# RMS norm of later queries and keys through a product with ones, ScalarE and GpSimd; modulation products spread over four FFN tiles

## The chip, the cores and the metric

The kernel runs on one core of a Trainium2 chip. The metric is the time of one execution on the device in microseconds (us), the median of several runs. A core has these engines: TensorE (PE, with its weight loads shown apart as PEld) multiplies matrices into PSUM; VectorE (DVE), ScalarE (ACT) and GpSimd (POOL) work elementwise; SyncE (SP) issues the DMAs here. Each engine works through its own queue in order and waits on semaphores for the others.

## The reference

Two layers work on 512 latent and 256 context tokens of width 1024. Layer 0 is grouped-query attention, layer 1 a bidirectional state-space mixer; behind each comes a gated FFN with a short convolution. Shift, scale and gate of each sub-layer come from `ada_w` and the condition vectors. The part that the change touches:

```python
def rms_norm(x, g):
    xf = x.astype(jnp.float32)
    y = xf * lax.rsqrt(jnp.mean(xf * xf, axis=-1, keepdims=True) + EPS)
    return (y * g.astype(jnp.float32)).astype(x.dtype)
...
    q_l, k_l, v_l = jnp.split(h_lat @ w_qkv, [Q_DIM, Q_DIM + KV_DIM], axis=-1)
    q_l = rms_norm(q_l.reshape(bsz, seq, N_HEADS, HEAD_DIM), q_norm)
    k_l = rms_norm(k_l.reshape(bsz, seq, N_KV_HEADS, HEAD_DIM), k_norm)
...
    q_l = apply_rope(q_l, cos, sin)
    k_l = apply_rope(k_l, cos, sin)
...
    for i in range(DEPTH):
        need_ctx_out = i < DEPTH - 1
        mod_l = jnp.split((silu_c @ ada_w[i] + ada_b[i])[:, None, :], 6, axis=-1)
        mod_c = jnp.split(silu_cc @ ada_w[i] + ada_b[i], 6, axis=-1)
```

There are 16 query heads and 4 key heads of 64; the norm runs over the 64 values of one head and token. EPS is 1e-6.

## The kernel before

Activations lie transposed: 128 features on the partitions, 768 tokens (512 latent, then 256 context) in the free dimension. A tile of 128 rows so holds two heads of 64 rows each. Linear layers run as three products in a reduced fp32 format: a weight tile and an activation are each split into a high and a low half (`split`, `load_w`: ACT makes the high half at L85, VectorE or GpSimd the low half at L87), and `mm3` adds high x high, high x low and low x high (L105 to L108).

The kernel is written for a framework that places instructions into the engines' queues at build time: by a priority, which is the order of the program's text, and by when it reckons that an instruction's inputs are ready. On the chip each queue then runs in this fixed order.

**Attention.** Eight pairs of heads `p` (one query tile each) go through seven steps each (`Pair.steps`): scores into PSUM (L668, L670), exponential on ACT (L671), sum of exponentials on VectorE (L678), and one step later the product with the values (L632). In the steps of pair p the maxima of pair p+1 are found too (`Pair.maxima`, L596 and L598), and for these the queries of pair p+1 must be normed and split. Scores and maxima share a PSUM ring of two buffers (`S`); all other products share four banks (`Bank`).

Into each step `Fill.run` puts other work from a queue of generators: the projection of later queries, their norm, the modulation products `ada` of layer 0 and, later, the output projection. A generator's `yield` says how much of the step's budget (1.75 us in pairs 0 to 5, 2.9 in 6 and 7) its piece used; a `yield BREAK` counts 1.0 and rests the generator until the third step after. `fill.require` (L738, L740) runs the rest of a generator on the spot if it isn't done when its pair needs it. The queue is written out as "123a4k5a6a7aaa" (L722): digits are queries, k the second tile of keys (needed from pair 3), a an `ada`.

**The norm.** `normed` (L520) squares the tile on ACT (`sq`, L523), applies the gain (L524), and rotates the positions: four DMAs on SP swap the rows (L527), and three operations on engine `eng` do the rotation (L528 to L530). `eng` is VectorE for key tile 0 and query tile 0, GpSimd for key tile 1 and query tiles 1 to 7. Then `rstd_rows` (L227): six small products with `blk`, which has one column for each head, put the sums of squares with tokens on the partitions (`ssq`, L236); VectorE scales them (L239); ACT takes Ln and Exp for the root (L241); VectorE makes one Newton step (L243, L244) and spreads the result over a head's 64 columns (`rbq`, L247); six transposes on TensorE bring it back to features on the partitions (`rsTq`, L253); VectorE multiplies (L534). The pieces are parted by BREAKs: three in a norm. Behind it `queries` splits the tile into `qh` and `ql` (L569), `keys` makes its copies (L545 to L548).

**FFN of layer 0 and the products of modulation.** `ffn` goes through 22 tiles `f` of the hidden width. `up(f)` makes two products (gate branch and up branch, each with its own weight), the convolution on VectorE (L832, L833), SiLU on ACT and the gating on VectorE (`hd`, L843), and its split (`hdh`, `hdl`). Tiles are collected in groups (3, then 2 at a time); the down-product of a group (`flush`, `down`) follows the first tile of the next group. Beside this runs the generator `side`, which is `ada_dve` (L153): the modulation of layer 0's FFN gate and of all of layer 1 as dot products on VectorE, 80 in all, each 1024 elements long (`junk`, L167). Each `next(side)` issues one. The first 16 make the gate that the first down-product's result is multiplied with (L779); a `modulation` (L145) follows them. `up(f)` takes `some` of them behind the SiLU and as many behind the second product (L835 to L840).

Of the kernel before, what the change touches and what calls it, by code (L numbers as in the profile page):

```python
# [7 lines left out]
P = 128  # L8
F32 = mybir.dt.float32
F32R = mybir.dt.float32r  # L10
AF = mybir.ActivationFunctionType
ALU = mybir.AluOpType
# [5 lines left out]
L = 512  # L18
C = 256
T = L + C  # L20
HD = 64
# [4 lines left out]
EPS = 1e-6  # L26
# [41 lines left out]
def t3(g, name, dt=F32, n=T):  # L68
    return g.t3p.tile([P, n], dt, tag="t3", bufs=g.n3, name=name)
# [103 lines left out]
BREAK = object()  # L173
# [53 lines left out]
def rstd_rows(g, sq, n, cols, width, name, bank):  # L227

    nc = g.nc
    c = cols.shape[-1]
    nt = n // P
    ps = bank(f"ss{name}")
    for t in range(nt):
        nc.tensor.matmul(ps[:, t * c : (t + 1) * c], sq[:, t * P : (t + 1) * P], cols, start=True, stop=True)  # L236
    small = lambda nm: g.p.tile([P, nt * c], F32, tag="rst", bufs=8, name=nm)
    a, y, u = small("rsa"), small("rsy"), small("rsu")
    nc.vector.tensor_scalar(a, ps[:, : nt * c], 1.0 / width, EPS, ALU.mult, ALU.add)  # L239

    for f in ((lambda: nc.scalar.activation(y, a, AF.Ln)), (lambda: nc.scalar.activation(y, y, AF.Exp, scale=-0.5))):  # L241
        follow(g, f()) if g.tables else f()
    nc.vector.tensor_tensor(u, y, a, ALU.mult)  # L243
    nc.vector.scalar_tensor_tensor(u, y, -0.5, u, ALU.mult, ALU.mult)  # L244
    rb = t3(g, f"rb{name}", n=n)
    wide = lambda v: v.unsqueeze(2).broadcast_to([P, nt * c, P // c])
    nc.vector.scalar_tensor_tensor(rb.rearrange("p (a b) -> p a b", b=P // c), wide(u), 1.5, wide(y), ALU.add, ALU.mult)  # L247
    yield BREAK
    out = []
    for t0 in range(0, nt, 4):  # L250
        pt = bank(f"rsT{name}")
        for t in range(t0, min(nt, t0 + 4)):
            nc.tensor.transpose(pt[:, (t - t0) * P : (t - t0 + 1) * P], rb[:, t * P : (t + 1) * P], g.ident)  # L253
        yield (pt, t0 * P, min(n, (t0 + 4) * P))
# [124 lines left out]
def attention(g, fill, X, late):  # L379


    nc, I = g.nc, g.I
    S64 = slice(0, 64), slice(64, 128)
# [123 lines left out]
    def values():  # L507
        for t in range(T // P):
# [7 lines left out]
                yield 0.32  # L516
            nc.scalar.copy(vt[t], ps[:, :256])


    def normed(qs, gain, eng):  # L520

        sq = t3(g, "qsq")
        nc.scalar.activation(sq, qs, AF.Square)  # L523
        nc.scalar.activation(qs, qs, AF.Identity, scale=gain)  # L524
        sw = t2("qsw")
        for b in range(4):
            nc.sync.dma_start(sw[32 * (b ^ 1) : 32 * (b ^ 1) + 32], qs[32 * b : 32 * b + 32, :L])  # L527
        eng.tensor_tensor(qs[:, :L], qs[:, :L], g.cos, ALU.mult)  # L528
        eng.tensor_tensor(sw, sw, g.sin, ALU.mult)
        eng.tensor_tensor(qs[:, :L], qs[:, :L], sw, ALU.add)  # L530
        for r in rstd_rows(g, sq, T, g.blk, HD, "q", Bk):
            if r is not BREAK:
                pt, c0, c1 = r
                nc.vector.tensor_tensor(qs[:, c0:c1], qs[:, c0:c1], pt[:, : c1 - c0], ALU.mult)  # L534
            yield BREAK
# [255 lines left out]
def ffn(g, layer, streams, x, h, first, nxt=None, side=iter(()), after=()):  # L791

    nc, I = g.nc, g.I
    ns = len(streams)
    tot = sum(n for n, _ in streams)
    off = [0, L]

    cw = [g.par[:, PC[f"fw{layer}{t}"] : PC[f"fw{layer}{t}"] + NFT] for t in range(3)]  # L800
    cb = g.par[:, PC[f"fb{layer}"] : PC[f"fb{layer}"] + NFT]
    whole = [[(i, 0, n) for i, (n, _) in enumerate(streams)]]

    def gemm(t):

        if t % NFT == 0:
            ps = first[t // NFT]
        else:
            w = load_w(g, I["wup"][layer, t])
            if t % NFT == 1:  # L810
                out = []
                for i in range(ns):
                    ps = Bank(g, "ps_up1")
                    for _ in gemm_in(g, [(ps, w)], h, (0, 0), [[s] for s in whole[0] if s[0] == i]):
                        pass
                    out.append((ps, [i]))
                return [(ps[:, : streams[i][0]], off[i], off[i] + streams[i][0], i) for ps, (i,) in out]
            ps = S(g, "ps_up")
            for _ in gemm_in(g, [(ps, w)], h, off, [[s] for s in whole[0]]):
                pass  # L820
        return [(ps[:, :tot], 0, tot, None)]

    def up(f):
        pg = gemm(f)
        cv = t3(g, "cv", n=tot)
        w0, w1, w2 = (c[:, f : f + 1] for c in cw)
        for ps, a, b, _ in pg:
            nc.scalar.activation(cv[:, a:b], ps, AF.Identity, scale=w1, bias=cb[:, f : f + 1])
        for i in range(ns):
            a, b = off[i], off[i] + streams[i][0]  # L830
            ps, o = next((ps, o) for ps, o, e, j in pg if j in (None, i))
            nc.vector.scalar_tensor_tensor(cv[:, a + 1 : b], ps[:, a - o : b - o - 1], w0, cv[:, a + 1 : b], ALU.mult, ALU.add)  # L832
            nc.vector.scalar_tensor_tensor(cv[:, a : b - 1], ps[:, a - o + 1 : b - o], w2, cv[:, a : b - 1], ALU.mult, ALU.add)  # L833
        follow(g, nc.scalar.activation(cv, cv, AF.Silu))
        some = 4 if ns > 1 and f < 2 else 1  # L835
        for _ in range(some):
            next(side, None)
        pu = gemm(NFT + f)
        for _ in range(some):
            next(side, None)  # L840
        hd = t3(g, "hd", n=tot)
        for ps, a, b, _ in pu:
            nc.vector.tensor_tensor(hd[:, a:b], cv[:, a:b], ps, ALU.mult)  # L843
        hi, lo = t3(g, "hdh", F32R, n=tot), t3(g, "hdl", F32R, n=tot)
        split(g, hd, hi, lo)
        return [(hi[:, off[i] : off[i] + streams[i][0]], lo[:, off[i] : off[i] + streams[i][0]]) for i in range(ns)]

    gate = g.mod[layer][5]
    segs, f = [], 0
    for n in [3] + [2] * 8 + [3] if nxt else [2] * 11:  # L850
        segs.append(range(f, f + n))
        f += n
    acts, pend, wf = {}, None, []

    def flush(fs, order, norm=None, after=None):
        ws = [load_w(g, I["wdown"][layer, f * P : (f + 1) * P]) for f in fs]
        if after:
            wf.extend(firsts(g, *after))
        return down(g, ws, [acts.pop(f) for f in fs], gate, streams, x, order, norm, side=side)

    for fs in segs:
        for j, f in enumerate(fs):
            acts[f] = up(f)
            if j == 0 and pend:
                flush(pend, whole)
        pend = fs
    for _ in side:
        pass
    if nxt:
        ln_exp(g)  # L870
    return flush(pend, [[s] for s in ending(streams)], nxt, after), wf
# [569 lines left out]
```

## Time and profile before

| | |
|---|---|
| Runs | 1917.7, 1918.88, 1925.51 us; median 1918.88 |
| Profiled execution | 1921.56 us, span of its trace 1919.8 us, mean granted TensorE clock 0.991 |
| TensorE, share of the span | 98% |
| VectorE | 68% |
| ScalarE | 43% |
| GpSimd | 16% |
| DMA, mean | 109 GB/s |

The attention stage lies at about 45 to 395 us, the FFN of layer 0 at about 445 to 965 us. In the rows, an operation stands with its line, its engine, its form (partitions x elements), its count, the time that the group kept the engine busy, the mean ns of one, and the idle time of the engine before it with what ended it. In the view of one tile three numbers are the least, the median and the longest ns. Rows of the timeline begin with start and length in us; those of the chain of waits too. TensorE's products overlap in its pipeline, so the length of one is longer than the distance to the next. A row of windows has the stretch, its length, the busy time of PE, PEld, DVE, ACT and POOL with the number of instructions, the granted clock, the DMA share and GB/s.

### The profile page before, as it was taken

To read this page: it belongs to the slowest core of one execution; us is meant where nothing else is said; L and a number is where in the kernel's file an instruction comes from. 1 tells how busy PE (TensorE), PEld (TensorE's weight loads), DVE (VectorE), ACT (ScalarE), POOL (GpSimd) and SP (SyncE) were. 2 spreads that over 40 slices of the span, in tenths; PEclk is the share of its full clock that TensorE was granted. 3 is DMA by queue.
4 is the path that set the end of the run, shared out by engine and by line. 5 is a ranking of instruction groups with operands and counts; after the bars stand their busy time and mean duration, and the time that the engine had idled before them with its cause. 6 is when DMAs were issued, how large, how long until landed. Compare 5 with 4: busy or idle time off the path is not lost.

```text
span 1919.8 us, 27433 instructions
## 1 busy us (share of the span) xinstructions
PE 1874.9 (98%) x10796; PEld 1545.7 (81%) x10796; DVE 1310.0 (68%) x1943; ACT 822.9 (43%) x1426; POOL 311.6 (16%) x274
## 2 busy tenths in 40 slices
PE   8999999999899999999999999999999999999999
PEld 6866555688788888888888888888888878888887
DVE  4577779678777777445578777777878466565555
ACT  3544444354222222222256767766667352323331
POOL 2241111031000000000030334443334210000000
PEclk8999999999999999999999999999999999999999
DMA  8221322014343554112222444344344322323232
GB/s 336 77 89 44 113 103 104 33 45 157 131 131 130 181 183 164 63 59 67 67 88 76 118 121 121 118 125 132 113 131 122 98 72 84 107 88 108 89 99 88
DMA packets 73425, 210.02 MB, mean 109 GB/s; under 512 B 8912, under 2 KB 14416, under 8 KB 73168
## 3 DMA queue, kind: packets, MB, share of 16 engines
q1 hardware_dynamic: 73296, 208.26, 33.6%
q8 instruction: 85, 1.39, 0.3%
q14 instruction: 44, 0.36, 0.1%
HBM read 198.79 MB, written 6.82 MB: 107 GB/s over the span
## 4 chain that ended last, share of the span: by engine, by line
PE 79%; DVE 10%; issue 3%; ACT 2%; POOL 1%; DMA 1%; SPq 0%; DVEq 0%; POOLq 0%; ACTq 0%
PE ps_up L108 10%; PE ps_up L106 10%; PE ps_up L105 10%; PE ps_d L105 6%; PE ps_d L106 6%; PE ps_d L108 6%; PE ps_in L108 4%; PE ps_in L106 4%; PE ps_in L105 4%; PE ps_o L632 2%; PE ps_s L668 2%; PE ps_st L1028 2%; DVE ht L281 1%; PE ps_wo L108 1%; PE ps_wo L105 1%
## 5 line engine op out<-in xcount | busy, mean ns | idle before, releaser
L87 DVE TENSOR_TENSOR wl<-wst,wh 128x1024 fp32r<-128x1024 f32 x205 | 255.9, 1248 | 241.1 <-PE ps_up L106 140.7
L85 ACT CAST wh<-wst 128x1024 fp32r<-128x1024 f32 x211 | 221.3, 1049 | 413.0 <-DMA wst<-in_wup 321.9
L108 PE MATMUL ps_up<-hhf,wl 128*128 128x512 f32 x1008 | 357.9, 355 | 5.0 <-DVE wl L87 5.0
L106 PE MATMUL ps_up<-hlf,wh 128*128 128x512 f32 x1008 | 357.9, 355 | 0.0
L105 PE MATMUL ps_up<-hhf,wh 128*128 128x512 f32 x1008 | 357.9, 355 | 0.0
L108 PEld LDWEIGHTS ps_up<-hhf,wl 128*128 128x128 f32 x1008 | 191.2, 190 | 32.3 <-DVE wl L87 5.5
L105 PEld LDWEIGHTS ps_up<-hhf,wh 128*128 128x128 f32 x1008 | 191.1, 190 | 26.8
L106 PEld LDWEIGHTS ps_up<-hlf,wh 128*128 128x128 f32 x1008 | 191.2, 190 | 26.7
L105 PE MATMUL ps_in<-hhs,wh 128*128 128x512 f32 (+1 forms) x560 | 204.4, 365 | 0.0
L106 PE MATMUL ps_in<-hls,wh 128*128 128x512 f32 (+1 forms) x560 | 199.4, 356 | 0.0
L108 PE MATMUL ps_in<-hhs,wl 128*128 128x512 f32 (+1 forms) x560 | 198.7, 355 | 0.0
L105 PE MATMUL ps_d<-hdh,wh 128*128 128x512 f32 (+1 forms) x568 | 193.4, 342 | 1.5 <-DVE X L779 1.3
L108 PE MATMUL ps_d<-hdh,wl 128*128 128x512 f32 (+1 forms) x568 | 193.4, 341 | 0.0
L106 PE MATMUL ps_d<-hdl,wh 128*128 128x512 f32 (+1 forms) x568 | 192.9, 340 | 0.3 <-DVE hdl L87 0.3
L779 DVE SCALAR_TENSOR_TENSOR X<-ps_d,mod,X 128x512 f32<-128x512 f32 (+1 forms) x224 | 125.3, 587 | 40.8 <-PE ps_d L108 40.5
L105 PEld LDWEIGHTS ps_d<-hdh,wh 128*128 128x128 f32 x568 | 106.3, 188 | 14.9 <-DVE X L779 1.5
L106 PEld LDWEIGHTS ps_d<-hdl,wh 128*128 128x128 f32 x568 | 106.7, 188 | 14.3 <-DVE hdl L87 0.7
L105 PEld LDWEIGHTS ps_in<-hhs,wh 128*128 128x128 f32 x560 | 105.9, 189 | 15.2 <-issue 1.2
L108 PEld LDWEIGHTS ps_in<-hhs,wl 128*128 128x128 f32 x560 | 105.8, 189 | 14.8
L108 PEld LDWEIGHTS ps_d<-hdh,wl 128*128 128x128 f32 x568 | 106.7, 188 | 13.1
L106 PEld LDWEIGHTS ps_in<-hls,wh 128*128 128x128 f32 x560 | 106.0, 189 | 13.2
L671 ACT ACTIVATE pr<-ps_s 128x1024 f32<-128x1024 f32 x56 | 57.2, 1022 | 107.7 <-PE ps_s L670 106.8
(340 smaller groups left out, 3542.7 us busy)
## 6 DMA issues: line engine op xcount, KB each, us to landing
wst<-in_wup SPq DMA_DIRECT2D x88, 512.0 KB, 3.5
wada<-in_adaT SPq DMA_DIRECT2D x56, 512.0 KB, 3.7
wst<-in_win SPq DMA_DIRECT2D x48, 512.0 KB, 3.6
wst<-in_wdown SPq DMA_DIRECT2D x44, 512.0 KB, 4.1
E<-ad SPq DMA_DIRECT2D x64, 256.0 KB, 7.5
wada<-in_adaB SPq DMA_DIRECT2D x24, 512.0 KB, 4.5
ec<-ead SPq DMA_DIRECT2D x64, 128.0 KB, 5.7
wst<-in_wout SPq DMA_DIRECT2D x16, 512.0 KB, 3.5
```

What stands on the lines that cost most here:

```text
L85: keep(nc.scalar.copy(hi, src))
L87: keep(eng.tensor_tensor(lo, src, _r(hi), ALU.subtract))
L105: mm(out, wh, ah, start=first, stop=False)
L106: mm(out, wh, al, start=False, stop=False)
L108: mm(out, wl, ah, start=False, stop=last)
L281: nc.vector.scalar_tensor_tensor(t[:, c0:c1], ap, g.moda[layer][ca][:, m, v : v + 1], rs[:, c0:c1], ALU.mult, ALU.mult)
L632: nc.tensor.matmul(po[S64[e], :n], v, pr[:, 512 * e + off : 512 * e + off + n], start=first, stop=last)
L668: nc.tensor.matmul(outs[e], a[S64[e], k], b[S64[e], q], start=i == 0, stop=False)
L671: nc.scalar.activation(pr, ps, AF.Exp)
L779: nc.vector.scalar_tensor_tensor(ap, o[:, c0:c1], gate[:, m, v : v + 1], ap, ALU.mult, ALU.add)
L1028: nc.tensor.matmul(ps[:, d * 256 : (d + 1) * 256], Bt[:, t * P : (t + 1) * P], xw[d][t], start=t == ts[0], stop=t == ts[-1])
```

## The change

Two parts. In `normed`, tiles on GpSimd get their own ending: four products with a 64x64 block of ones (`g.ones[h, :HD]`) sum a head's squares straight onto all of the head's 64 rows, with the tokens still in the free dimension; ACT brings them from PSUM with the factor 1/64 and EPS; Ln, Exp, Square and the last linear step of the Newton iteration run on ACT over all 768 columns, three products on GpSimd. The transposes and VectorE's part fall away, and so does one of three BREAKs. Two small constants are set by GpSimd for the activations' biases. Key tile 0 and query tile 0 keep the old way.

In `ffn` of layer 0, the tiles 0 to 3 take 2, 2, 2 and 3 products of modulation at each of their two places, where the tiles 0 and 1 took 4 and all others 1.

```diff
@@ -516,6 +516,10 @@
             nc.scalar.copy(vt[t], ps[:, :256])
 
+    eps, c15 = (g.const.tile([P, 1], F32, name=n) for n in ("eps", "c15"))
+    nc.gpsimd.memset(eps, EPS)
+    nc.gpsimd.memset(c15, 1.5)
+
 
     def normed(qs, gain, eng):
 
@@ -528,6 +532,26 @@
         eng.tensor_tensor(qs[:, :L], qs[:, :L], g.cos, ALU.mult)
         eng.tensor_tensor(sw, sw, g.sin, ALU.mult)
         eng.tensor_tensor(qs[:, :L], qs[:, :L], sw, ALU.add)
+        if eng is nc.gpsimd:
+            a, y = t3(g, "qa"), t3(g, "qy")
+            for c in (slice(0, L), slice(L, T)):
+                ps = Bk("ssq")[:, : c.stop - c.start]
+                for h in S64:
+                    nc.tensor.matmul(ps[h], g.ones[h, :HD], sq[h, c], start=True, stop=True)
+                nc.scalar.activation(a[:, c], ps, AF.Identity, scale=1.0 / HD, bias=eps)
+            yield BREAK
+            u = sq
+            nc.scalar.activation(y, a, AF.Ln)
+            nc.scalar.activation(y, y, AF.Exp, scale=-0.5)
+            nc.scalar.activation(u, y, AF.Square)
+            eng.tensor_tensor(u, u, a, ALU.mult)
+            eng.tensor_tensor(qs, qs, y, ALU.mult)
+            nc.scalar.activation(u, u, AF.Identity, scale=-0.5, bias=c15)
+            eng.tensor_tensor(qs, qs, u, ALU.mult)
+            yield BREAK
+            return
         for r in rstd_rows(g, sq, T, g.blk, HD, "q", Bk):
             if r is not BREAK:
                 pt, c0, c1 = r
@@ -832,7 +856,7 @@
         follow(g, nc.scalar.activation(cv, cv, AF.Silu))
-        some = 4 if ns > 1 and f < 2 else 1
+        some = (2, 2, 2, 3)[f] if ns > 1 and f < 4 else 1
         for _ in range(some):
             next(side, None)
         pu = gemm(NFT + f)
```

## The prediction

> **What bounds the kernel now.** I read the page's totals first, then the chain of waits, then busy times by windows in the two stages that the change touches.
>
> ```profile
> PE 1874.9 (98%) x10796; PEld 1545.7 (81%) x10796; DVE 1310.0 (68%) x1943; ACT 822.9 (43%) x1426; POOL 311.6 (16%) x274
> PE 79%; DVE 10%; issue 3%; ACT 2%; POOL 1%; DMA 1%; SPq 0%; DVEq 0%; POOLq 0%; ACTq 0%
> ```
>
> TensorE is the bound: 98% busy and 79% of the chain. So work taken from VectorE pays only where TensorE stands for it; work taken from TensorE pays in full wherever it runs without a break. The windows of the attention stage are cut about where a pair of heads ends (the row "sum" covers seven of them, 97 to 311 us):
>
> ```profile
> 128.00:155.00 27.00, 26.16 (x170) 14.63 (x168) 23.25 (x33) 11.01 (x17) 8.99 (x6) 0.89 0.29 96
> ...
> 278.00:311.00 33.00, 31.47 (x226) 15.85 (x223) 29.31 (x46) 15.69 (x21) 5.67 (x3) 1.00 0.45 160
> sum 214.00, PE 208.56 PEld 126.89 DVE 168.18 ACT 92.91 POOL 47.18; mean PE 29.79 PEld 18.13 DVE 24.03 ACT 13.27 POOL 6.74
> ```
>
> The columns are window, length, then PE, weight loads, DVE, ACT and POOL busy, and the granted clock. TensorE is busy 208.56 of 214 us. VectorE has 168.18 us, but 29.31 of 33 in the last window and 23.25 of 27 in the first: there it is nearly a second bound. ACT is at 43% (92.91 of 214), GpSimd at 22% (47.18). A step is 3.9 to 4.7 us (27 and 33 us, seven steps each).
>
> **TensorE's products in the norm.** The change touches eight norms (queries 1 to 7 and the second block of keys; the two early ones run on VectorE and stay). Each loses six fp32 products with `blk` (12 instructions, two passes each) and six transposes. It gains four products with a 64x64 stationary of ones: two heads by 512 columns, two heads by 256. No row shows a 64x64 product. The nearest are the sums of the softmax at L638, also fp32 and with ones, two heads on the two column halves, 512 and 256 columns wide. The chain gives all of them:
>
> ```profile
> 195.63 0.59 PE rsTq L253 x4
> ...
> 207.48 0.37 PE rsTq L253 x2
> ...
> 210.23 0.86 PE ps_sum L638 x4
> 211.09 1.43 PE ssq L236 x12
> 212.52 1.85 PE ps_ada L128 x16
> ...
> 216.51 0.43 PE ps_oc L638 x4
> ```
>
> Removed per norm: 1.43 + 0.59 + 0.37 = 2.39 us. Added: 0.86 + 0.43 = 1.29. That is 1.10 us less. The chain books the tail of one block to the next, which moves each price by about a tenth (the same block of twelve starts at 211.09 and the one after it at 212.52, but three blocks become two), so I take 0.9 us, times 8: **-7.2 us**. Bounds: -8.8 (1.10 x 8) if nothing is lost; if the two heads' products don't run side by side, the added part is 2 x 1.29 = 2.58, and the term is +1.5 (0.19 x 8).
>
> A rule of the Trainium skill speaks against the lower price. Its page "TensorEngine Tiling (Array Packing)", section "Restrictions and Gotchas", says that different row tiles can't use one PSUM bank at the same time, and here both heads' products (rows 0 to 63 and 64 to 127) write one bank. By it the term would be the +1.5 just named. The rows of L638 share a bank too, but have all 128 rows, so they don't test it; in this kernel the 64-row products of L668 write two banks. It is a rival below.
>
> **ScalarE, VectorE, GpSimd in the norm.**
>
> ```profile
> L523 ACT ACTIVATE qsq<-qs 128x768 f32<-128x768 f32 x4 | 3.4, 846 | 0.1
> ...
> L565 ACT COPY qs<-ps_q 128x512 f32<-128x512 f32 x4 | 2.3, 586 | 5.7 <-PE ps_q L108 5.7
> L517 ACT COPY v<-ps_v 128x256 f32<-128x256 f32 x6 | 2.2, 372 | 12.1 <-PE ps_v L515 12.1
> ...
> L241 ACT ACTIVATE rsy<-rsa 128x12 f32<-128x12 f32 x10 | 2.1, 212 | 15.0 <-DVE rsa L239 14.9
> ```
> ```profile
> L243 DVE TENSOR_TENSOR rsu<-rsy,rsa x21: 150/170/2084, 14.2 to 1554.3; 128x12 f32<-128x12 f32 x10, 128x2 f32<-128x2 f32 x9, 128x4 f32<-128x4 f32 x2
> L244 DVE SCALAR_TENSOR_TENSOR rsu<-rsy,rsu x21: 161/164/1193, 14.4 to 1555.0; 128x12 f32<-128x12 f32 x10, 128x2 f32<-128x2 f32 x9, 128x4 f32<-128x4 f32 x2
> L247 DVE SCALAR_TENSOR_TENSOR rbq<-rsu,rsy x10: 949/959/2052, 79.3 to 297.0; 128x768 f32<-128x768 f32 x10
> ```
> ```profile
> L534 DVE TENSOR_TENSOR qs<-qs,rsTq x8: 416/550/689, 197.1 to 308.2; 128x512 f32<-128x512 f32 x4, 128x256 f32<-128x256 f32 x4
> ```
> ```profile
> L529 POOL TENSOR_TENSOR qsw<-qsw,cs x8: 1266/1285/2267, 103.7 to 291.2; 128x512 f32<-128x512 f32 x8
> ...
> L530 POOL TENSOR_TENSOR qs<-qs,qsw x4: 1273/2174/2182, 180.6 to 293.5; 128x512 f32<-128x512 f32 x4
> ```
>
> ACT gains two evictions (0.59 and 0.37) and four activations of 768 (0.85 each) and loses two small ones (0.21 each): 0.96 + 3.40 - 0.42 = 3.94 us a norm, 31.5 us in eight, so it goes from 43% to 58% of that stretch. VectorE loses three small operations (0.17 each, L239 being of L243's size), `rbq` (0.96) and the two products with the transposed rows (0.69 and 0.42): 2.58 us a norm, 20.6 us in all. GpSimd gains three products of 768. By 512 columns at 1.29 us alone and 2.17 in contention (medians of L529 and L530), 768 are 1.9 to 3.3 us; eight norms add 46 to 78 us to its 47, which 214 us hold. L243 at its longest (2.08 us for 12 elements, median 0.17) shows the price of the other side: VectorE stands while a GpSimd product holds something that both need. If each of the 24 new products makes VectorE wait half its length, that is 23 us or more, so I count VectorE's relief as given back and the contention as paid by it: 0, bounds -2.5 (the whole wait for `ma` below) and +3.
>
> Is the longer arithmetic late for anyone? The second part of a norm (Ln, Exp, Square, three GpSimd products, one Identity) lasts 3 x 0.85 + three products: 8.3 to 12.5 us; the Identity hides beside the second product. The queue `Fill` decides when it is issued: a BREAK takes 1.0 of the step's 1.75 us and rests the generator until the third step after. I worked the queue "123a4k5a6a7aaa" through with both sets of yields (three BREAKs a norm before, two after). Before, the last parts of queries 2, 4, 5, 6 and 7 are left to `fill.require`, right ahead of the pair that needs them. After, one BREAK less leaves none: the second part always comes three steps (12 to 14 us) before the split, and the split itself one to seven steps before its pair. So the chain is covered, with little to spare when GpSimd is slow; if the cover went, each norm's 8 to 12 us would stand before its pair.
>
> **Waits in this stage.**
>
> ```profile
> PE ps_m L596 <- DVE ma L598: 2.5, 4, 0.8
> PE rsTq L253 <- DVE rbq L247: 2.0, 1, 2.0
> ```
> ```profile
> ACT rsy L241 <- DVE rsa L239: 12.0, 6, 3.7
> ```
>
> TensorE's one wait of 2.0 us for `rbq` goes with the transposes: **-2.0**. ACT no longer stands 12.0 us for `rsa`, with exponentials of scores behind it; in its place it can stand at the new Identity, which waits for GpSimd's product, again with exponentials behind, and TensorE behind these. The trace shows no such wait. Lower bound -1 (the old wait's cost gone, no new one), upper +8 (one us lost in each norm); I take **+1.5**, nearer to the old wait's small effect. The longer life of `a`, `y` and `sq` (three of 18 `t3` buffers across the break where `rbq` was one) can delay a norm's start, not a pair; it is in those bounds. The two memsets run while GpSimd idles.
>
> With a BREAK less, the three last `ada` products (1.85 us each at L128) move from pair 5 into pair 4. Pair 5 (the window 278 to 311) then has 31.47 - 5.6 - 2.4 = 23.5 us for TensorE, while VectorE keeps 29.31 - 2.6 - three small copies, about 25: **+1.2** (0 to +3).
>
> **The modulation's products.**
>
> ```profile
> 485.49:492.31 6.82, 5.26 (x12) 4.13 (x13) 3.18 (x5) 2.09 (x2) 0.00 (x0) 0.50 0.65 231
> 454.60:487.00 32.40, 27.41 (x163) 24.10 (x161) 31.94 (x53) 9.15 (x12) 0.00 (x0) 0.98 0.50 163
> 487.00:506.00 19.00, 18.95 (x95) 16.41 (x96) 9.38 (x12) 4.88 (x6) 0.00 (x0) 0.86 0.32 113
> ```
> ```profile
> L167 DVE SCALAR_TENSOR_TENSOR junk<-wada,cb x80: 1212/1220/1232, 454.7 to 760.2; 128x1024 f32<-128x1024 f32 x80
> ```
> ```profile
> 481.65 0.95 DVE L843 TENSOR_TENSOR hd<-cv,ps_up 128x768 f32<-128x768 f32 x1 [0.33 <-PE ps_up L108]
> ...
> 485.77 1.22 DVE L87 TENSOR_TENSOR wl<-wst,wh 128x1024 fp32r<-128x1024 f32 x1
> ```
> ```profile
> 487.05 0.80 PE L108 MATMUL ps_up<-hhf,wl 128*128 128x512 f32 x1 [5.03 <-DVE wl L87]
> ```
>
> VectorE is busy 31.94 of 32.40 us ahead of 487, with 18 of the 80 products in it, and the low half `wl` of the next weight comes so late that TensorE stands 5.03 us; the clock then drops to 0.50, and 5.26 us of work run at half speed, 2.6 us lost: 7.6 in all. After, by the code, 4 + 4 + 4 = 12 products instead of 8 + 8 + 2 come before that point, 6 x 1.22 = 7.3 us less, so `wl` can go ahead of `hd`. Four of the six land in the fourth tile (6 there instead of 2), two later. VectorE had 9.6 us free there (19.00 - 9.38), but without the stall the stretch is 19.00 - 7.6 = 11.4 us, in which it must do 9.4 + 4.9: not all fits, and what doesn't runs earlier or delays a weight of the first down-product. I take **-6.5**; bounds -7.6 and -3.5. Their loads move later in SP's queue with them, behind weights, and are then wanted later too; I count nothing for them. The change adds no DMA.
>
> **Sum.** -7.2 - 2.0 + 1.5 + 1.2 - 6.5 = -13.0 us. The profiled execution took 1921.56 us, with a span of 1919.8; the median of the three runs is 1918.88. I take the difference from the median: **1906 us**, own range 1899 to 1912.
>
> **Rivals.**
> - The two heads' products run one after the other: +1.5 instead of -7.2, so 1914.6. For it: one bank, which no row tests. Against it: all pairs in this trace that differ in rows or in columns overlap (L638's four instructions, two heads by two passes, take 0.86 us, as two passes alone would if 1.85 us hold the sixteen of L128, four at a time).
> - The wait for `wl` moves on to the first down-product and takes back 4 us: 1910. For it: the 11.4 us above; against it: 9.6 us of free time that the stall itself had hidden.
> - The steps don't get shorter, because VectorE with GpSimd's contention sets them; only the FFN's part and the 2.0 remain, less the 1.5 and 1.2 lost: 1918.9 - 6.5 - 2.0 + 2.7 = 1913. For it: 29.31 of 33 in pair 5; against it: 168 of 214 over all.
> - Slower: ACT's in-order queue stands at the Identity behind a slow GpSimd product with another ahead of it: 3.3 + 1.9 = 5.2 us a norm, less some 1.0 that TensorE's other work in a step covers, 4.2 x 8 = 33.6 in place of 1.5: 1938. It decides from 1.8 us a norm on (14.5 / 8). For it: L530's median of 2.17 against 1.29 alone, so a planned order is easily early; against it: the three steps between the parts, and only exponentials that fall into the gap are hit.
> - The change does not do what it says: the products land in the queue as before and TensorE still waits at `wl`; that is the second rival at its far end.
>
> **How the numbers follow.** Forecast 0.50, heads one after the other 0.12, wait moved 0.15, steps set by VectorE 0.13, slower 0.10. About 0.5% (9.6 us) can be told from no change, so faster means below 1909.3. Of the forecast nine tenths lie there, of the moved wait half, of the two others little: 0.45 + 0.08 + 0.04 = 0.57. Slower takes the 0.10, the rest is 0.33. The range: all favourable bounds together (-8.8 - 2.5 - 2.0 - 1 - 7.6 = -21.9) would give 1897, and since they will hardly all meet I cut at 1899; the upper end takes in the rivals at 1910, 1913 and 1914.6 and some 4 us more of ACT's term: 1919.
>
> **What would show it.** `ssq` should read about 1.3 us a norm on the chain, and no `rsTq` behind queries 1 to 7; twice that would be the bank rival. No wait of TensorE over 1 us at 480 to 500 us, and no clock of 0.50 there. ACT's waits should name GpSimd at the Identity for under 2 us a norm; more, with exponentials of scores late behind it and TensorE standing at L668, would make the prediction wrong. A wait of `ps_m` for the split of the next queries would say that the cover of three steps is gone.

## The result, and the profile after

| | before | after |
|---|---|---|
| Median of the runs made side by side | 1919.72 us (1917.7 to 1925.51, 4 runs) | 1936.29 us (1934.85 to 1937.47, 4 runs) |
| Ratio, 95% interval | | 1.0093 [1.0075, 1.0112] |
| Profiled span | 1919.8 us | 1933.9 us |
| Mean granted TensorE clock | 0.991 | 0.988 |

The change makes the kernel 16.6 us slower. The page of the changed kernel shows the engines' busy time, and below it the chain by engine:

```profile
PE 1872.3 (97%) x10716; PEld 1535.3 (79%) x10716; DVE 1293.5 (67%) x1895; ACT 852.7 (44%) x1458; POOL 358.8 (19%) x300
...
PE 75%; DVE 8%; POOL 4%; issue 4%; ACT 3%; DMA 1%; SPq 0%; POOLq 0%; DVEq 0%; ACTq 0%
```

Each engine's total moved as planned: TensorE and VectorE work less, ScalarE 30 us more, GpSimd 47 us more. But TensorE's part of the chain fell from 79% to 75% and GpSimd's rose from 1% to 4%: GpSimd's work has come onto the path.

Where? The last instruction of a pair of heads reads `ps_oc`; the view of that tile gives the first and the last start of it. First the kernel before, then the changed one:

```profile
L643 DVE TENSOR_TENSOR o<-ps_oc,y x8: 416/420/426, 158.4 to 393.9; 128x256 f32<-128x256 f32 x8
```
```profile
L667 DVE TENSOR_TENSOR o<-ps_oc,y x8: 416/424/425, 167.0 to 416.7; 128x256 f32<-128x256 f32 x8
```

Attention ends 22.8 us later, the span only 14.1 us: behind attention 8.7 us are won. So there are two results of opposite sign. The windows of the changed kernel (columns as in the prediction) show both:

```profile
97.00:336.00 239.00, 208.75 (x1288) 116.45 (x1286) 154.72 (x197) 126.33 (x169) 94.69 (x52) 0.94 0.27 88
...
500.00:516.00 16.00, 16.00 (x95) 14.20 (x94) 11.16 (x16) 4.49 (x5) 0.00 (x0) 1.00 0.44 132
```

The first row covers the same part of the program as the 214 us before (208.56 us busy there): the end of the preparation and pairs 0 to 5. TensorE's busy time is equal, so its idle time went from 5.4 to 30.3 us; the time of the products that it was spared is spent again at a lower granted clock (0.94 against 0.98 over the stretch). In slices of 3 us the clock falls to between 0.50 and 0.67 behind each of the six stalls of 2.4 us or more. The second row lies where the 5.03 us stall of the FFN was (22 us later now): no gap, and full clock.

What ScalarE and TensorE stood for from 95 to 337 us (waits: who, for what; us in total, times, longest):

```profile
ACT qh L85 <- POOL qs L552: 16.4, 4, 7.0
ACT qsq L551 <- POOL qsq L549: 16.0, 8, 3.9
...
ACT qh L85 <- POOL raw L552: 4.4, 2, 4.1
ACT wh L85 <- POOL wl L87: 4.2, 1, 4.2
...
ACT qy L546 <- POOL raw L550: 3.4, 1, 3.4
```
```profile
PE ps_s L692 <- ACT pr L695: 19.7, 8, 5.4
PE ssq L542 <- ACT qsq L527: 5.0, 1, 5.0
PE ps_s L694 <- DVE diag L643: 4.6, 4, 2.0
PE ps_m L620 <- DVE ma L622: 1.0, 1, 1.0
```

ScalarE stands 44.4 us for GpSimd. In the kernel before it stood for none of GpSimd's work in the pairs, but 12.0 us for VectorE's `rsa` and 8.8 us at the casts of queries, for VectorE too. More than half of the 44.4 us is not at the Identity (L551) but at casts (L85), above all those of the normed queries (`qs` and `raw`, 20.8 us in six waits). TensorE's main wait, 19.7 us, is for ScalarE's exponentials; the kernel before had none of it. The timeline shows how the one makes the other:

```profile
268.04 1.85 POOL L549 TENSOR_TENSOR qsq<-qsq,qa 128x768 f32<-128x768 f32 x1 [28.82 <-ACT qsq L548]
...
269.86 2.26 POOL L532 TENSOR_TENSOR qs<-qs,cs 128x512 f32<-128x512 f32 x1
269.93 0.94 ACT L551 ACTIVATE qsq<-qsq,c 128x768 f32<-128x768 f32 x1 [1.05 <-POOL qsq L549]
...
271.35 1.02 ACT L695 ACTIVATE pr<-ps_s 128x1024 f32<-128x1024 f32 x1 [0.48 <-PE ps_s L694]
...
273.44 2.15 POOL L534 TENSOR_TENSOR qs<-qs,qsw 128x512 f32<-128x512 f32 x1
...
274.75 0.50 PE L692 MATMUL ps_s<-qh,kh 64*128 64x512 f32 x2
...
275.55 0.39 PE L694 MATMUL ps_s<-diag,onesr 64*128 64x512 f32 x2
275.67 1.81 POOL L550 TENSOR_TENSOR qs<-qs,qy 128x768 f32<-128x768 f32 x1
...
277.56 1.80 POOL L552 TENSOR_TENSOR qs<-qs,qsq 128x768 f32<-128x768 f32 x1
279.39 0.83 ACT L85 CAST qh<-qs 128x768 fp32r<-128x768 f32 x1 [7.02 <-POOL qs L552]
...
282.46 1.00 ACT L695 ACTIVATE pr<-ps_s 128x1024 f32<-128x1024 f32 x1
...
283.51 0.80 PE L692 MATMUL ps_s<-qh,kh 64*128 64x512 f32 x2 [5.35 <-ACT pr L695]
```

In GpSimd's queue the rope of the same queries (L532 to L534) stands between the norm's first product and its second, 5.8 us of it. The cast is the next instruction in ScalarE's queue after the exponential at 271.35; it waits 7.02 us, and the following exponential, whose scores were done at 276, waits behind it and three short instructions. TensorE has both score buffers full and stands 5.35 us. Its next products are slower: the pair at 283.51 takes 0.80 us against 0.50 at 274.75, and the granted clock is 0.50 from 283 to 289.

At other norms the Identity is the place. From the chain of the changed kernel, start, length, engine and tile:

```profile
194.22 1.99 POOL qs L550
196.21 1.82 POOL qsq L549
198.03 0.02 issue
198.05 0.94 ACT qsq L551
198.99 0.07 issue
199.06 1.82 POOL qs L552
```

Here `qs*y` even runs ahead of `u*a`, so the Identity waits for two products.

### The profile page after: what moved, and what is told of

Its sections match the earlier page's. It is cut to its first block, busy times and chain, and to the rows that moved or that the text cites. A ratio compares the mean times of both kernels' runs of the same rounds, so it can differ in the third digit from the quotient of the medians.

```text
span 1933.9 us, 27320 instructions
## 1 busy us (share of the span) xinstructions
PE 1872.3 (97%) x10716; PEld 1535.3 (79%) x10716; DVE 1293.5 (67%) x1895; ACT 852.7 (44%) x1458; POOL 358.8 (19%) x300
## 4 chain that ended last, share of the span: by engine, by line
PE 75%; DVE 8%; POOL 4%; issue 4%; ACT 3%; DMA 1%; SPq 0%; POOLq 0%; DVEq 0%; ACTq 0%
PE ps_up L106 10%; PE ps_up L108 10%; PE ps_up L105 10%; PE ps_d L105 6%; PE ps_d L106 6%; PE ps_d L108 6%; PE ps_in L108 4%; PE ps_in L106 4%; PE ps_in L105 4%; PE ps_s L692 2%; PE ps_o L656 2%; PE ps_st L1052 2%; DVE ht L281 1%; PE ps_wo L108 1%; PE ps_wo L105 1%
## 5 line engine op out<-in xcount | busy, mean ns | idle before, releaser
L85 ACT CAST wh<-wst 128x1024 fp32r<-128x1024 f32 x211 | 221.2, 1049 | 428.9 <-DMA wst<-in_wup 338.3
L330 POOL TENSOR_TENSOR sqs<-sqs 128x256 f32<-128x256 f32 x15 | 11.2, 743 | 523.7 <-issue 516.7
```

Source lines behind the costliest of these rows:

```text
L85: keep(nc.scalar.copy(hi, src))
L330: (nc.vector if m == 7 else nc.gpsimd).tensor_tensor(acc, acc, sq, ALU.add)
```

## The experiments

Each is a variant of the kernel before or of the changed one; the time is the median, and the difference is against the median of the kernel before in the runs made beside it. "Excess" is worked out from the records of 97 to 340 us: the length of each VectorE instruction with two operands in SBUF, less the shortest of its form, summed.

**1. The FFN part alone.** The kernel before with the new spread only:

```diff
-        some = 4 if ns > 1 and f < 2 else 1
+        some = (2, 2, 2, 3)[f] if ns > 1 and f < 4 else 1
```

> The kernel before with only the modulation's products spread 2, 2, 2, 3 over the first four channel groups of the FFN; the norm is left as it was, and all of the reference is computed. The theory (the loss lies in attention, where ScalarE's queue stands behind GpSimd's products) expects the FFN's gain alone: the stall of 5.03 us at the first up-product and the 3.4 us that the half clock behind it costs go, so some 1912 us, 7 to 8 us under the kernel before, and an attention stage that ends at 392 us as before. If the spread itself brought the loss, this run is above 1925 us.

Measured: 1910.89 us, -7.3, ratio 0.996 [0.9948, 0.9973]. The window of this run where TensorE stood before has no gap:

```profile
485.00:492.00 7.00, 7.00 (x42) 6.20 (x41) 4.49 (x6) 2.97 (x3) 0.00 (x0) 1.00 0.29 85
```

So the new norm by itself costs some 24 us (16.6 + 7.3), and everything below is about the norm.

**2. The norm's products on VectorE.**

```diff
-            eng.tensor_tensor(u, u, a, ALU.mult)
-            eng.tensor_tensor(qs, qs, y, ALU.mult)
+            nc.vector.tensor_tensor(u, u, a, ALU.mult)
+            nc.vector.tensor_tensor(qs, qs, y, ALU.mult)
             nc.scalar.activation(u, u, AF.Identity, scale=-0.5, bias=c15)
-            eng.tensor_tensor(qs, qs, u, ALU.mult)
+            nc.vector.tensor_tensor(qs, qs, u, ALU.mult)
```

> The changed kernel with the three products of the Newton step (u*a, qs*y, qs*u) issued on VectorE and not on GpSimd; the rope's products stay on GpSimd, ScalarE's work and the order of the fill's pieces stay, and all of the reference is computed. Theory (ScalarE stands in its order at the Identity and at the cast of qs behind GpSimd's products of 1.8 to 2.8 us, the exponentials of the scores stand behind it, and TensorE behind these): the waits of ScalarE on GpSimd in the stretch of the pairs fall from some 32 us to under 8, the attention stage ends near 395 us, the time is 1900 to 1914 us. Rival, ScalarE's added work of some 31 us is itself the loss: the time stays at 1928 to 1940. Rival, the thinner fill of pair 5 and the order of the pieces: the time stays at 1928 to 1940. Rival, GpSimd and VectorE slow each other: gains as the theory does, and the run with the products on GpSimd held back tells the two apart.

Measured: 1915.75 us, -2.4, ratio 0.9993 [0.9979, 1.0007], a little above the range expected; attention ends at 394.4. TensorE's wait for exponentials falls from 19.7 to 5.5 us, and some 19 of the 24 us come back with three products moved. The rivals of ScalarE's work and of the fill's order fall, since both are as in the changed kernel.

**3. ScalarE held back, the products left on GpSimd.** `held` adds an order of ScalarE's queue only; REST and PAUSE rest the generator two steps:

```diff
-            nc.scalar.activation(u, u, AF.Identity, scale=-0.5, bias=c15)
+            yield REST
+            held(g, nc.scalar.activation(u, u, AF.Identity, scale=-0.5, bias=c15))
             eng.tensor_tensor(qs, qs, u, ALU.mult)
-            yield BREAK
+            yield PAUSE
...
+            held(g, nc.scalar.copy(hi, qs))
```

> The changed kernel with its products left on GpSimd, but the Identity and the casts of the normed rows are put, in ScalarE's order, behind the exponentials that the program has issued by then, with pauses of two steps ahead of the Identity and ahead of the casts, so that GpSimd has time to finish. All of the reference is computed. Theory (what costs is the place in ScalarE's order, not GpSimd's speed): ScalarE's waits on GpSimd fall from some 32 us to under 10 and the time is at most 1914 us. Rival, ScalarE's added work: stays at 1928 to 1940. Rival, GpSimd and VectorE slow each other: stays at 1925 to 1940, since GpSimd does the same products beside the same VectorE work. Rival, the fill is too thin: 1936 or more, since the pauses make it thinner.

Measured: 1928.11 us, +9.9, ratio 1.0051 [1.0036, 1.0066]. ScalarE's waits for GpSimd fell from 44.4 to 17.0 us, but only 7 us came back: my theory of that point, that the place in ScalarE's queue is the whole loss, missed. The excess of VectorE is 21.3 us here against 10.0 in the changed kernel.

**4. The whole step on VectorE, without the Identity.**

```diff
-            eng.tensor_tensor(u, u, a, ALU.mult)
-            eng.tensor_tensor(qs, qs, y, ALU.mult)
-            nc.scalar.activation(u, u, AF.Identity, scale=-0.5, bias=c15)
-            eng.tensor_tensor(qs, qs, u, ALU.mult)
+            nc.vector.tensor_tensor(u, u, a, ALU.mult)
+            nc.vector.scalar_tensor_tensor(u, u, -3.0, y, ALU.add, ALU.mult)
+            nc.vector.scalar_tensor_tensor(qs, u, -0.5, qs, ALU.mult, ALU.mult)
```

> The changed kernel with the Newton step as three VectorE instructions, u*a, then (u - 3)*y, then (that times -0.5)*qs, so that neither GpSimd's products nor ScalarE's Identity are left in the norm; Ln, Exp and Square stay on ScalarE. All of the reference is computed, by the same algebra. Theory: ScalarE has no instruction left that reads a product of the norm but the cast, which reads VectorE's; its waits there fall under 5 us, and the time is 1899 to 1912 us, the same as or a little under the run with the three products on VectorE and the Identity kept. Rival, ScalarE's added work: it loses only the Identity, 0.94 us of some 4 us a norm, so the time is 1925 or more. Rival, VectorE becomes the bound of the pairs (three products of 768 columns more a norm): above the run with the products on GpSimd held back.

Measured: 1913.62 us, -4.6, ratio 0.9975 [0.9965, 0.9985], a little above the range expected.

**5. Dead products on GpSimd.** Experiment 4 plus GpSimd work that nobody reads:

```diff
+            for _ in range(4):
+                eng.tensor_tensor(sw, sw, g.sin, ALU.mult)
```

> The run with the whole Newton step on VectorE, with GpSimd's work put back as dead work: four products of 512 columns a norm (sw*sin into sw, some 5.1 us against the 5.4 us of the three products of the changed kernel) whose results nobody reads, issued in front of VectorE's step. All of the reference is computed. ScalarE waits for none of these products; they only occupy GpSimd, its queue, and what it shares with VectorE. Theory A (ScalarE's place in its order is the whole loss): 1912 to 1919 us. Theory B (besides, GpSimd's products and VectorE's sums of two operands in SBUF hold each other up: the sum of the exponentials took 2.0 to 2.8 us beside such a product and 1.22 us alone): 1921 to 1932 us, with the sum of the exponentials at 2 us or more some ten times in the pairs.

Measured: 1933.85 us, +16.1, ratio 1.0078 [1.0048, 1.0108]. Products that nobody reads cost 20.7 us over experiment 4, somewhat more than theory B allowed. It stands, but not by the instruction that I had named: only three sums of exponentials exceed 1.9 us. The small VectorE instructions ahead of the scores are hit, and the excess is 28.8 us against 10.5 in experiment 4. Timeline of the run:

```profile
153.41 6.28 POOL L550 TENSOR_TENSOR qsw<-qsw,cs 128x512 f32<-128x512 f32 x4
...
153.80 2.79 DVE L639 TENSOR_TENSOR mz<-ma,mb 64x6 f32<-64x6 f32 x4
...
156.62 1.94 DVE L87 TENSOR_TENSOR ql<-raw,qh 128x768 fp32r<-128x768 f32 x1
```

Four products of six elements take 2.79 us, and TensorE then waits for `diag` (10.6 us in five waits of this run). The tile views say the same; first this run, then the next:

```profile
L639 DVE TENSOR_TENSOR mz<-ma,mb x32: 148/160/1248, 110.4 to 370.6; 64x6 f32<-64x6 f32 x32
...
L644 DVE TENSOR_TENSOR diag<-id,mz x16: 544/553/2755, 113.2 to 371.2; 128x384 fp32r<-128x384 f32 x16
```

**6. Dead memsets in place of the dead products.**

```diff
-            for _ in range(4):
-                eng.tensor_tensor(sw, sw, g.sin, ALU.mult)
+            for _ in range(10):
+                eng.memset(sw, 0.0)
```

> The run with dead GpSimd products, with these four products replaced by ten memsets of 512 columns of the same tile: GpSimd's queue is occupied for about as long (its duration is read from the trace), but it reads nothing from SBUF. All of the reference is computed. Theory B (the shared read of SBUF holds VectorE's two-operand instructions up): VectorE's instructions keep their undisturbed times beside the memsets, and the time is 1911 to 1919 us, near the 1913.6 without dead work. Rival C (what stands behind the dead work in GpSimd's queue, the rope of the next norm and the low parts of the weights, comes late): the time stays at 1925 to 1935 us, as with the products.

Measured: 1917.06 us, +0.1, ratio 0.9992 [0.9977, 1.0007].

```profile
L550 POOL MEMSET qsw<- 128x512 f32 x80 | 41.6, 526 | 3.9
```
```profile
L639 DVE TENSOR_TENSOR mz<-ma,mb x32: 147/160/164, 110.9 to 354.9; 64x6 f32<-64x6 f32 x32
...
L644 DVE TENSOR_TENSOR diag<-id,mz x16: 548/551/561, 111.6 to 355.6; 128x384 fp32r<-128x384 f32 x16
```

GpSimd is held for 41.6 us, which is what 32 products of 1.28 us alone would take; in experiment 5 they took 53.0 us, since they were held up too. What stands behind the memsets in GpSimd's queue comes nearly as late, and this costs 3 to 5 us over experiment 4. The other 16 us of experiment 5 are there only if GpSimd reads SBUF. Without that no `mz` or `diag` is lengthened, and the excess is 12.0 us. The Trainium skill, page "SBUF — State Buffer", section "Who interferes with whom", says it so: a VectorE instruction with two SBUF inputs contends with a GpSimd instruction that reads SBUF, not with one that only writes it. This pair of runs agrees; so does VectorE's maximum of a PSUM tile (1.21 to 1.23 us in every run).

**7. One product moved, or the other two.** First `u*a` alone on VectorE, then `qs*y` and `qs*u`:

```diff
-            eng.tensor_tensor(u, u, a, ALU.mult)
+            nc.vector.tensor_tensor(u, u, a, ALU.mult)
```

> The changed kernel with the first product, u*a, alone issued on VectorE, so that ScalarE's Identity waits for VectorE and not for GpSimd; qs*y and qs*u stay on GpSimd, and so the cast of qs still waits for GpSimd. All of the reference is computed. Theory A: the Identity's waits (16 us in the changed kernel's pairs) fall to some 7 and the cast's (16 us) stay, 1922 to 1930 us. Rival, the Identity is where all is lost: 1916 or less. Rival, the cast is where all is lost: 1932 or more.

Measured: 1931.44 us, +13.7, ratio 1.0068 [1.0047, 1.009].

```diff
-            eng.tensor_tensor(qs, qs, y, ALU.mult)
+            nc.vector.tensor_tensor(qs, qs, y, ALU.mult)
...
-            eng.tensor_tensor(qs, qs, u, ALU.mult)
+            nc.vector.tensor_tensor(qs, qs, u, ALU.mult)
```

> The complement: qs*y and qs*u issued on VectorE, u*a left on GpSimd; the Identity still waits for GpSimd, the cast for VectorE. All of the reference is computed. Theory A: the cast's waits fall to some 8 us and the Identity's stay at 16, 1922 to 1930 us. Theory B gives less, 1917 to 1926, since two of three products have left GpSimd. Rival, the Identity is where all is lost: 1932 or more. Rival, the cast is where all is lost: 1918 or less.

Measured: 1922.32 us, +4.6, ratio 1.0019 [1.0004, 1.0034]. Against the 16.6 of the changed kernel, one product off GpSimd is worth 2.9 us, two 12.0, all three 19.0. The first run lies above theory A's range, just under the 1932 at which the cast would be all; the second is in the range of both theories. They don't divide the loss between Identity and cast. In the first, 14.4 us of the 16.4 at the cast of `qs` are left, but the Identity still stands 11.7 of its 16.0 us, now for VectorE. In the second, 14.7 of the Identity's 16.0 are left, and the casts of queries go from 20.8 to 10.0 us. The second run also takes two products from beside VectorE, the first only one.

**8. Without the Newton step.** Ln straight from the sums' bank, Exp, one product on VectorE:

```diff
-                nc.scalar.activation(a[:, c], ps, AF.Identity, scale=1.0 / HD, bias=eps)
+                nc.scalar.activation(y[:, c], ps, AF.Ln, scale=1.0 / HD, bias=eps)
             yield BREAK
...
-            nc.scalar.activation(y, a, AF.Ln)
             nc.scalar.activation(y, y, AF.Exp, scale=-0.5)
...
+            nc.vector.tensor_tensor(qs, qs, y, ALU.mult)
```

> The changed kernel's sums by products with ones onto a head's rows, with a lighter root: Ln on ScalarE straight from the sums' bank, Exp on ScalarE, one product qs*y on VectorE. The Newton step on the root is left out, so the last digits of the norm differ. ScalarE loses some 3.8 us of work a norm against the changed kernel, GpSimd its three products, VectorE gains one product of 768 columns, and nothing on ScalarE but the cast waits for a product of the norm. If the sums' saving on TensorE (0.78 us for each of eight norms) is real and the rest can be hidden: 1902 to 1908 us, under the run with the FFN part alone. Rival, the pairs' steps are set by VectorE and ScalarE and TensorE's saving is given back as waits: 1909 to 1914 us, no better than the FFN part alone.

Measured: 1911.4 us, -6.3, ratio 0.9963 [0.9945, 0.9981]. The lightest norm on the new sums can't be told from the FFN part alone (0.996).

**9. Dead work on ScalarE.** Experiment 8 with three Squares of 768 more in each norm:

```diff
+            for _ in range(3):
+                nc.scalar.activation(sq, sq, AF.Square)
```

> The run without the Newton step (1911 us), with three dead Squares of 768 columns a norm put back on ScalarE (some 0.84 us each, 2.5 us a norm, 20 us in all), which nobody reads and which wait for nothing but ScalarE and the sums. The Newton step stays left out. Theory (ScalarE's added work is not what costs): 1909 to 1915 us. Rival, ScalarE's added work costs by itself: 1920 us or more.

Measured: 1915.78 us, -1.2, ratio 0.9987 [0.9974, 1.0001]. Twenty us of ScalarE work cost about 5, a little more than the theory allowed and below the rival. About as much of the 24 us is left in experiment 2; whether it is the same loss isn't shown.

**10. Held back without the pauses.** Experiment 3 with BREAK in place of PAUSE, and no REST:

```diff
-            yield REST
-            yield PAUSE
+            yield BREAK
```

> The changed kernel with the Identity and the casts of the normed rows put behind the exponentials issued by then, as in the run held back, but without the pauses, so that the fill of the pairs is that of the changed kernel. All of the reference is computed. Theory A (ScalarE's place in its order is the whole loss, and the pauses spoilt the run held back): at most 1916 us. Theory D (GpSimd's products cost in either place: ScalarE waits for them, or, where it doesn't, they run beside VectorE's sums and both take longer): 1922 to 1934 us, with VectorE's two-operand instructions some 15 us or more over their undisturbed times, against 10 us in the changed kernel.

Measured: 1922.3 us, +5.3, ratio 1.0025 [1.0012, 1.0039]. So the pauses did spoil experiment 3 in part, and 11.3 us of the changed kernel's loss go with ScalarE's order alone. The rest stays. Theory D had the time at its lower end, but the excess (14.0 us) is just under what it asked for, and ScalarE still stands 23.7 us for GpSimd, so the rest isn't shown to be contention alone. One stall with contention ahead of it shows at the end of pair 5, in the timeline:

```profile
296.42 2.22 DVE L87 TENSOR_TENSOR wl<-wst,wh 128x1024 fp32r<-128x1024 f32 x1
...
297.63 2.66 POOL L560 TENSOR_TENSOR qs<-qs,qy 128x768 f32<-128x768 f32 x1
298.56 1.76 DVE L148 SCALAR_TENSOR_TENSOR moda<-mod,par 128x8 f32<-128x8 f32 x1
300.24 1.21 DVE L719 TENSOR_TENSOR acc<-acc,pr 128x1024 f32<-128x1024 f32 x1
300.38 2.75 POOL L562 TENSOR_TENSOR qs<-qs,qsq 128x768 f32<-128x768 f32 x1
...
301.38 1.21 DVE L639 TENSOR_REDUCE ma<-ps_m 128x2 f32<-128x1024 f32 x1
```

An eight-element VectorE instruction takes 1.76 us and ends with GpSimd's product; that product takes 2.66 us, not 1.8. The maximum comes late, and TensorE waits 4.6 us for it.

**11. The rope on VectorE as well.** To see whether GpSimd's older products cost in the same way, the rope's three were moved in the FFN-only kernel and in experiments 8 and 4:

```diff
-        eng.tensor_tensor(qs[:, :L], qs[:, :L], g.cos, ALU.mult)
-        eng.tensor_tensor(sw, sw, g.sin, ALU.mult)
-        eng.tensor_tensor(qs[:, :L], qs[:, :L], sw, ALU.add)
+        nc.vector.tensor_tensor(qs[:, :L], qs[:, :L], g.cos, ALU.mult)
+        nc.vector.tensor_tensor(sw, sw, g.sin, ALU.mult)
+        nc.vector.tensor_tensor(qs[:, :L], qs[:, :L], sw, ALU.add)
```

In the FFN-only kernel:

> The kernel with the FFN part alone (1910.9 us), its norm as before, and the rope's three products of 512 columns moved from GpSimd to VectorE. All of the reference is computed. If GpSimd's products and VectorE's sums hold each other up in the kernel before too (VectorE's two-operand instructions exceed their undisturbed times by some 9 us there, the rope's products by some 7), then 1903 to 1909 us; if VectorE's added work of some 16 us costs as much as that or the excess was hidden, 1910 to 1916 us.

Measured: 1909.1 us, -7.9, ratio 0.9958 [0.9943, 0.9973], against 0.996 [0.9948, 0.9973] without the move: no difference that can be told. Either the older, smaller load of GpSimd was hidden, or VectorE's added work costs what its absence saves.

Without the Newton step:

> The run without the Newton step, with the rope's three products moved to VectorE as well, so that GpSimd does almost nothing in the pairs. The Newton step stays left out. If GpSimd's remaining products were what ate TensorE's saving: 1902 to 1907 us. If the saving is given back in the steps of the pairs whatever GpSimd does (TensorE then waits for VectorE's maxima and for ScalarE's exponentials): 1909 to 1914 us, as without the move.

Measured: 1909.87 us, -8.1, ratio 0.9949 [0.993, 0.9969], within the range of a saving that is given back.

With the whole step on VectorE:

> The run with the whole Newton step on VectorE, with the rope's three products moved there as well. All of the reference is computed. VectorE then carries some 5 us more a norm than in the kernel before, and GpSimd next to nothing. If only GpSimd beside VectorE costs: 1904 to 1910 us. If VectorE's load becomes the bound of the pairs: 1913 to 1920 us.

Measured: 1915.22 us, -2.8, ratio 0.9983 [0.9971, 0.9995]. With GpSimd almost idle and VectorE carrying everything, the complete new norm is no better than experiment 4. The time is where VectorE's load as the bound would put it, but TensorE's waits there are shared: 6.0 us for VectorE and 5.8 for ScalarE.

The FFN part beside them:

> The FFN part alone once more, on the same chip as the two runs with the rope on VectorE, so that differences under half a per cent are read on one chip: 1908 to 1913 us. All of the reference is computed.

Measured: 1910.42 us, -7.6, ratio 0.9952 [0.9933, 0.9971].

Of the versions that compute all of the reference, the FFN part alone is the one to keep (0.996 and 0.9952 in two sets of runs): 0.4 to 0.5% faster than the kernel before, faster than the changed one, and none with the new norm is ahead of it; with the rope moved it is level (0.9958). The version without the Newton step and with the rope moved is level with it in the times; its one profiled execution was its fastest (1905.45 us, attention's last instruction at 386.3 against 393.6 in the FFN part beside it, which was profiled in its slowest, 1912.62 us), so whether a few us of TensorE's saving come through there stays open.

## Why the prediction was wrong

**The step that failed** is ScalarE's term: "I take **+1.5**", with bounds of -1 and +8, resting on "the second part always comes three steps (12 to 14 us) before the split" and "So the chain is covered, with little to spare when GpSimd is slow". In the changed kernel TensorE waits 19.7 us for exponentials that come late, and of the 24 us that the norm costs, 11.3 go when only ScalarE's order is changed (experiment 10). Three things were missing.

First, the three steps are not in ScalarE's queue. Query 4 in the changed kernel, Ln, Identity and cast, with the exponentials of the scores (L695) about them:

```profile
192.37 0.83 ACT L546 ACTIVATE qy<-qa 128x768 f32<-128x768 f32 x1
...
193.98 1.01 ACT L695 ACTIVATE pr<-ps_s 128x1024 f32<-128x1024 f32 x1
...
198.05 0.93 ACT L551 ACTIVATE qsq<-qsq,c 128x768 f32<-128x768 f32 x1 [1.61 <-POOL qsq L549]
200.91 0.83 ACT L85 CAST qh<-qs 128x768 fp32r<-128x768 f32 x1 [1.93 <-POOL qs L552]
201.65 1.02 ACT L695 ACTIVATE pr<-ps_s 128x1024 f32<-128x1024 f32 x1
```

A step has one exponential. Between the Identity and the cast stand 0, 0, 1 and 2 of them for queries 4 to 7. In experiment 10, which ties both to the exponentials issued by then, there are 3 for each of these queries. So the program's text kept the three steps, and the framework's order drew the cast forward.

Second, the chain was priced with GpSimd's queue to itself, 5.7 to 9.9 us for its three products. The rope can stand between them: at 268 us it took 11.4 us from the start of `u*a` to the cast, 5.8 of them rope. Third, only the Identity was looked at: the casts of queries wait longer (20.8 us in six waits, 7.0 at most, against 16.0) and hold up the exponentials just as well. The sign named for a lost cover, a wait of `ps_m` for the split, hardly came (0.9 us, once): the loss went by the exponentials.

**The contention**, "0, bounds -2.5 ... and +3", rests on a sum that doesn't hold. I set 23 us of VectorE's waiting against its relief of 20.6. But VectorE's time isn't one pool: experiment 5 shows waiting lands on the small instructions (`mz`, `diag`) that TensorE's scores stand behind, while the relief is spread. Experiments 5 and 6 price it at 16 us for about the amount of reading that the new norm does, where ScalarE waits for none of it. What it costs in the changed kernel isn't shown: there no `mz` or `diag` is lengthened (164 and 559 ns at most), and the excess is 10.0 us, under the 13.4 of the kernel before. That would fit a VectorE that idles beside the products while ScalarE waits; with ScalarE held back, the excess rises to 14.0 and 21.3. The two losses share one cause, GpSimd's products, and can't be added.

**The slower rival** named ScalarE's queue behind a slow product with another ahead of it, and 1938 us; 1936.29 came. Its mechanism is shown, and the chain at 194 us is that case to the letter. It is not the whole: the Identity makes 16.0 of ScalarE's 44.4 us, and the size of 33.6 us came near by luck, as what it left out (the casts, the lower clock) stood in for what it put in too high. Its chance of 0.10 was too low: the row that spoke for it, 2.17 us where a product alone takes 1.29, weighed more than the three steps against it.

**TensorE's products**, -7.2: the price was right. On the chain of the changed kernel a norm's sums read

```profile
217.87 1.44 PE ssq L542 x8
```

so 2.39 - 1.44 = 0.95 us less a norm, against 0.9 taken. The two heads do run side by side: the eight passes would take 2.58 us one after the other, and the records show the two of each pair starting 6 to 7 ns apart, in one bank. The rival of the shared bank falls; here the trace differs from the rule of the Trainium skill's page "TensorEngine Tiling (Array Packing)", section "Restrictions and Gotchas", that different row tiles can't use one PSUM bank at the same time. What failed is that the saving pays "in full wherever it runs without a break": experiment 8 has it and gains nothing that can be told. Its TensorE waits 8.3 us in all from 95 to 337 us, for VectorE and ScalarE in turn, against 3.6 in the FFN part alone:

```profile
PE ps_s L688 <- DVE diag L637: 2.4, 3, 1.7
PE ps_m L614 <- DVE mb L616: 2.0, 1, 2.0
PE ssq L542 <- ACT qsq L527: 1.9, 1, 1.9
```

The third rival, that VectorE and contention set the steps and only the FFN's part remains, fits that run. **The wait for `rbq`**, -2.0, is gone as said.

**Pair 5's thinner fill**, +1.2: not tried by itself. It is bounded by experiment 8, which has the same fill and is level with the FFN part.

**The FFN part**, -6.5: right in mechanism, 7.3 and 7.6 us measured, with no stall and no half clock at its place. It came to about the lower bound of -7.6, so that `wl` of the first down-product took nothing back; that rival falls.

## What to carry to other kernels

Before work goes to an engine that looks idle, follow the result back: which in-order queue holds the instruction that reads it, and what stands behind that one. A share of busy time says nothing of that; here GpSimd, 22% busy in this stretch before and 40% after, became the path, since ScalarE's exponentials queued behind the instructions that read its results. Steps of distance in the program's text are not steps in an engine's queue: read the order from the trace. Where VectorE is on the path, count GpSimd's products that read SBUF as VectorE time too, and weigh it by VectorE's shortest urgent instruction, not by its total.

## What was not expected of the hardware

A VectorE product of six elements took 160 ns as a rule and up to 1248 ns beside GpSimd's products of two SBUF operands; beside GpSimd's memsets it took at most 164 ns. The hold-up works both ways: GpSimd's product of 768 columns took 1.8 us alone and up to 2.8 us beside VectorE instructions of two SBUF operands. And work nobody waits for was not free on either engine: 53 us of dead GpSimd products cost 20.7 us, 20 us of dead ScalarE work about 5.
